# Gate and up products with tokens stationary and 512 weight columns moving, and TensorE transposes of the gated product

## The chip, the cores and the metric

The kernel runs on one core of one Trainium2 chip, in one launch. The metric is the device time of an execution in microseconds (us). TensorE (PE) multiplies matrices: one operand is loaded into the array and stands still (stationary), the other streams through it (moving). VectorE (DVE), ScalarE (ACT) and GpSimd (POOL) do the elementwise work, and SyncE (SP) issues most DMAs. Each engine has its own queue and takes its instructions in order.

## The reference

One layer of a hybrid encoder over 256 tokens of width 2048: two recurrent token mixers, cross attention over 256 memory tokens, and a gated feed forward of inner width 5632. Each part adds to the residual and ends in a layer norm. The change lies in the feed forward:

```python
def swiglu(h, wg, wu, wd):
    return (jax.nn.silu(h @ wg) * (h @ wu)) @ wd
...
        xa = memory_cross_attention(h, mem, xa_wq[l], xa_wk[l], xa_wv[l], xa_wo[l])
        h = layer_norm(ALPHA * h + xa, ln2_g[l], ln2_b[l])
        ff = swiglu(h, ffn_wg[l], ffn_wu[l], ffn_wd[l])
        h = layer_norm(ALPHA * h + ff, ln3_g[l], ln3_b[l])
```

`wg` and `wu` are 2048 x 5632, `wd` is 5632 x 2048, all float32.

## The kernel before

All large weights are streamed from memory once, in **units** of 128 partitions x 1024 columns (512 KB). For each unit `split_half` loads the raw float32 weights (L150, SP's queue, 4 buffers `raw`), rounds them to a high part `wh` on ACT (L153, 3 buffers), and subtracts to get the low part `wl` on DVE (L155, 3 buffers). The activations are kept as such pairs too (`xTh`, `xTl`: 16 pairs of tiles of 128 features x 256 tokens). A product is then three matmuls: high by high, high by low, low by high.

There are two forms of it. **`wstat`** (L164, L165, L168) has the weights stationary, 128 columns at a time, and 256 tokens moving. One unit is 8 tiles of the contraction for 128 output features, and so 24 matmuls of 256 moving columns: 16 that read `wh`, then 8 that read `wl`. The output has features on the partitions. **`xstat`** (L192, L193, L196) has 128 tokens stationary and 512 weight columns moving. One unit is two tiles of the contraction for 512 output features, for each of two halves of the tokens, and so 12 matmuls of 512 moving columns; the first four read `wh`, the next two `wl`, and then again for the other tokens. The output has tokens on the partitions.

The feed forward loops over 44 blocks of 128 inner features. For each it calls `wtile` (which calls `wstat`) for the gate and again for the up product (two units each, 176 in all), applies Silu on ACT (L888), multiplies on DVE (L890), and splits the product into the pair `fh`, `fl` (`split_to`: L201 on ACT, L202 on DVE). These lie with features on the partitions, which is how the down product needs its stationary operand: four calls of `xstat` over `wd`, 22 units each (88 in all), in which contraction tile k of `fh` and `fl` is read in rising k. `residual` (L782) and a closing layer norm follow.

Ahead of the feed forward stands the layer norm `g2`, `b2` (called LN2 below). It normalises `hres`, transposes it on PE in blocks of 128 x 128 into PSUM tiles `lnt` (L240, 4 buffers), scales into `lnfull` on DVE or ACT, and makes `xTh` and `xTl` tile by tile. `affine_rows` then multiplies `hres` by rows of gains that are broadcast by DMA into `gb` (L256, issued on ACT's queue, 2 buffers) on DVE (L258, L259); in the feed forward it is called after the second block, and nothing needs it before the down product ends.

A scheduler orders each engine's queue: `stream()` gives a unit's load and split the priority of the unit's place in the stream, so that the splits run about three units ahead of PE, as far as their buffers go. `defer(n, fn)` puts `fn` aside, and `passed`, called after each unit's matmuls, counts it down and issues it after n more units. Before the change only `wstat` calls `passed`.

Of the kernel before, what the change touches and what calls it, by code (L numbers as in the profile page):

```python
# [11 lines left out]
F32 = mybir.dt.float32  # L12
F32R = mybir.dt.float32r
# [5 lines left out]
P = 128  # L19
# [27 lines left out]
def trunk(ctx, tc, x, memT, vec, rows, consts, lruw, loraw, w_in, w_out, wq, wk, wv, wo, wgu, wd, out,  # L47
# [52 lines left out]

    # ---------------------------------------------------------------- constants
    vt = base.tile([P, NV], F32, name="vt")
# [41 lines left out]

    # ---------------------------------------------------------------- streamed products
    def split_half(src, hf):
# [32 lines left out]
    def xstat(srcs, xh, xl):  # L179
        pt = [new_acc(), new_acc()]  # L180
        n = len(srcs)
        for u, src in enumerate(srcs):
            for hf in range(2):
                h, l = split_half(src, hf)
                first = u == 0 and hf == 0
                last = u == n - 1 and hf == 1
                for tt in range(2):
                    ts = slice(tt * P, (tt + 1) * P)
                    for kk in range(2):
                        k = u * 4 + hf * 2 + kk  # L190
                        w = h[:, kk * 512:(kk + 1) * 512]
                        nc.tensor.matmul(pt[tt], xh[k][:, ts], w, start=(first and kk == 0), stop=False)  # L192
                        nc.tensor.matmul(pt[tt], xl[k][:, ts], w, start=False, stop=False)  # L193
                    for kk in range(2):
                        k = u * 4 + hf * 2 + kk
                        nc.tensor.matmul(pt[tt], xh[k][:, ts], l[:, kk * 512:(kk + 1) * 512],  # L196
                                         start=False, stop=(last and kk == 1))
        return pt
# [9 lines left out]

    # ---------------------------------------------------------------- layer norm
    def ln_stats(st, pre, tt, nb):  # L210
# [49 lines left out]

    # ================================================================ input norm
    h0_d = dram.tile([P, 2, 2048], F32, name="h0_d")
    xTh, xTl = pair_tiles(base, NK, "xT")
    # ================================================================ mixer
    ya_d = [dram.tile([P, T], F32, name=f"ya_d{k}") for k in range(NT)]
# [3 lines left out]
    with ExitStack() as mx:  # L269
# [13 lines left out]

        # ---- first memory keys while the input is normalised
        xt = boot.tile([P, 2, 2048], F32, name="xt")
# [50 lines left out]

        # ---- persistent buffers with zeroed parts
        bz = grp.tile([P, 2, 4, P], F32, name="bkz")
# [18 lines left out]

        # ---- low-rank inputs
        lo = [grp.tile([P, T], F32, name=f"lo{j}") for j in range(4)]
# [10 lines left out]
        def decay_rates(g, jp, rates):  # L370
            # ---- decay and in-context rate, two tiles
            if jp == 0:
# [52 lines left out]
        def tile_stage(g, j, i, u, fs, av, ev, dt, kr, bkt, sv, yb, gt):  # L425
# [3 lines left out]
            def key_direction():  # L429
                # even chunk: [r'|kk'], [k''|b']; odd chunk: [kk'|r'], [b'|k'']  # L430
                zk = z["k"]
# [77 lines left out]
        def recurrence(g, kkr, gt, bkt, sv, dm, yb, scr, scx, pace):  # L509
            # ---- (I + A_b)^-T  # L510
            gi = gt.rearrange("p i h c n -> p (i h) c n")
# [37 lines left out]
        def chunk_steps(g, kkr, gt, bkt, sv, dm, yb, gi):  # L549
# [23 lines left out]
            dump(f"ymat{g}", ymat)  # L573
            # ---- chunk recurrence
            smat = grp.tile([P, 512], F32, name="smat", tag="t2a")
            ott = grp.tile([P, 2, 512], F32, name="ott", tag="t4")
            ot = [ott[:, a] for a in range(2)]
            for c in range(4):
# [38 lines left out]
                nc.scalar.copy(ot[c // 2][p0:p0 + 64, :], pso[p0:p0 + 64, :])  # L617
            # ---- group norm by token
            for a in range(2):
# [155 lines left out]

    # ================================================================ attention
    mp = ctx.enter_context(tc.tile_pool(name="mps2", bufs=4, reuse_waits="tile", space=PSUM))
# [7 lines left out]
    with at:  # L785
# [12 lines left out]
        layer_norm(hres, st, "g1", "b1", mp, xTh, xTl, sm_, ("f0", "f1", "f2"))  # L798
        # memory keys and values
        mTh, mTl = pair_tiles(ap1, NK, "B")  # L800
# [78 lines left out]

    # ================================================================ feed forward  # L880
    with ExitStack() as fx:
        fp = fx.enter_context(tc.tile_pool(name="ffn", bufs=1, reuse_waits="tile"))
        fs_ = fx.enter_context(tc.tile_pool(name="ffs", bufs=2, reuse_waits="tile"))
        fh, fl = pair_tiles(fp, NF, "f")
        for f in range(NF):
            ag = wtile(wgu[2 * f], xTh, xTl)
            sg = fs_.tile([P, T], F32, name="fsg")
            last = nc.scalar.activation(sg, ag, AF.Silu)  # L888
            au = wtile(wgu[2 * f + 1], xTh, xTl)
            nc.vector.tensor_tensor(sg, sg, au, ALU.mult)  # L890
            split_to(sg, fh[f], fl[f])
            if f == 1:
                affine_rows(hres, 4, "gb2")
                dump("h2", hres)
# [53 lines left out]
def _layout(i):  # L948
# [47 lines left out]
    o["wo"] = _pack_x(a["xa_wo"][0])  # L996
    gu = np.stack([a["ffn_wg"][0].reshape(D, NF, P), a["ffn_wu"][0].reshape(D, NF, P)], axis=2)
    o["wgu"] = _pack_w(gu.reshape(D, 2 * DFF))
    o["wd"] = _pack_x(a["ffn_wd"][0])
# [23 lines left out]
```

## Time and profile before

| what | us |
|---|---|
| median of 3 runs (lowest, highest) | 2201.14 (2199.56, 2203.24) |
| span of the profiled execution, first to last instruction | 2197.7 |
| gate and up products, from LN2's first product to the first down product | 1429.6 to 1940.9 |
| down products | 1940.9 to 2180 |
| after the last product | 2180 to 2197.7 |

The runs are timed without the profile and lie 1.9 to 5.5 us above the profiled execution's span, which leaves out what lies before the first and behind the last instruction. A span that changes by some us is therefore set against the median by its difference. In the rows below, PE is a matmul and PEld the load of its stationary operand. A matmul's duration in a row is longer than its share of the engine, since the next one starts before it ends: the share is read from start to start. A matmul's names stand as `out<-moving,stationary`, and the shape at its end is the output's.

### The profile page before, as it was taken

What the parts mean: (1) busy time and instruction counts of PE and PEld (TensorE: products, weight loads), DVE (VectorE), ACT (ScalarE), POOL (GpSimd) and SP (SyncE); (2) the same over time, 40 slices, a digit from 0 to 9 for tenths busy, and PEclk for the clock granted to TensorE, in tenths of its full rate; (3) what the DMA queues carried; (4) which work ended last, traced back from release to release, by engine and by line L of the source; (5) the groups of instructions that cost most, each with busy time, mean ns of one, the idle gap of its engine ahead of it and who ended that gap; (6) DMA issues with size and microseconds to landing.
All of it is one profiled execution on the core that took longest, in us unless ns stands there. A gap on an engine that the chain in (4) does not pass through costs nothing.

```text
span 2197.7 us, 38943 instructions
## 1 busy us (share of the span) xinstructions
PE 2127.7 (97%) x15952; PEld 2004.9 (91%) x15952; DVE 1394.3 (63%) x2121; ACT 1031.9 (47%) x1442; POOL 102.8 (5%) x137
## 2 busy tenths in 40 slices
PE   7999999999999999989999999999999999999996
PEld 7999899999999999877988998799999999988885
DVE  7778676967695769567854555674444444444445
ACT  6646444554455445554544444354444444443332
POOL 1200010011001100200100000000000000000001
PEclk9999999999999999999999999999999999999998
DMA  8555445554555465467565545566555555555563
GB/s 301 186 166 172 140 130 171 177 153 139 176 168 154 139 180 183 123 223 247 183 206 194 165 140 165 190 198 200 184 182 183 184 184 183 182 188 194 192 193 124
DMA packets 149939, 392.41 MB, mean 179 GB/s; under 512 B 39296, under 2 KB 58624, under 8 KB 149248
## 3 DMA queue, kind: packets, MB, share of 16 engines
q1 hardware_dynamic: 137776, 368.81, 52.6%
q10 hardware_dynamic: 9296, 13.24, 2.4%
q0 software_dynamic: 2688, 7.87, 1.2%
q8 instruction: 125, 2.05, 0.4%
q14 instruction: 54, 0.44, 0.1%
HBM read 375.05 MB, written 10.62 MB: 175 GB/s over the span
## 4 chain that ended last, share of the span: by engine, by line
PE 82%; DVE 8%; DMA 6%; issue 2%; ACT 2%; ACTq 0%; POOL 0%; SPq 0%; DVEq 0%; POOLq 0%
PE acc L168 17%; PE acc L165 17%; PE acc L164 17%; PE acc L193 7%; PE acc L192 7%; PE acc L196 7%; DVE wl L155 3%; DVE pd L534 2%; DMA gb<-in_rows_dram 1%; PE mix L491 1%; DVE xi L537 1%; PE rec L590 1%; PE rec L615 1%; DMA bkz<-bk 1%; PE rec L597 1%
## 5 line engine op out<-in xcount | busy, mean ns | idle before, releaser
L155 DVE TENSOR_TENSOR wl<-raw,wh 128x1024 fp32r<-128x1024 f32 x656 | 800.7, 1222 | 581.9 <-ACT wh L153 539.7
L153 ACT CAST wh<-raw 128x1024 fp32r<-128x1024 f32 x656 | 687.4, 1049 | 869.6 <-PE acc L165 535.2
L164 PE MATMUL acc<-xTh,wh 128*128 128x256 f32 x3520 | 881.1, 287 | 1.5 <-DVE ge L694 0.8
L165 PE MATMUL acc<-xTl,wh 128*128 128x256 f32 x3520 | 875.7, 285 | 1.2 <-DVE xTl L248 0.8
L165 PEld LDWEIGHTS acc<-xTl,wh 128*128 128x128 f32 x3520 | 677.9, 193 | 4.5 <-DVE xTl L248 1.2
L164 PEld LDWEIGHTS acc<-xTh,wh 128*128 128x128 f32 x3520 | 677.3, 193 | 4.8 <-DVE ge L694 1.4
L168 PE MATMUL acc<-xTh,wl 128*128 128x256 f32 x3520 | 503.8, 284 | 1.3 <-DVE wl L155 1.3
L168 PEld LDWEIGHTS acc<-xTh,wl 128*128 128x128 f32 x3520 | 457.0, 192 | 3.6 <-DVE wl L155 2.1
L193 PE MATMUL acc<-wh,fl 128*128 128x512 f32 x352 | 136.9, 389 | 0.0
L192 PE MATMUL acc<-wh,fh 128*128 128x512 f32 x352 | 136.9, 389 | 0.0
L196 PE MATMUL acc<-wl,fh 128*128 128x512 f32 x352 | 108.4, 389 | 0.0
L196 PEld LDWEIGHTS acc<-wl,fh 128*128 128x128 f32 x352 | 66.1, 188 | 13.8
L193 PEld LDWEIGHTS acc<-wh,fl 128*128 128x128 f32 x352 | 66.1, 188 | 13.7
L192 PEld LDWEIGHTS acc<-wh,fh 128*128 128x128 f32 x352 | 66.0, 188 | 13.6
L534 DVE TENSOR_TENSOR pd<-xi,al 128x2 f32<-128x2 f32 (+30 forms) x124 | 63.0, 508 | 2.4
L603 POOL TENSOR_SCALAR dms<-ct,dm 128x128 f32<-128x128 f32 x48 | 39.1, 826 | 496.4 <-DVE smat L609 423.3
L890 DVE TENSOR_TENSOR fsg<-fsg,acc 128x256 f32<-128x256 f32 x44 | 18.5, 420 | 61.9 <-PE acc L168 61.4
L192 PE MATMUL acc<-wh,Ah 128*128 128x512 f32 x128 | 50.6, 395 | 0.0
L193 PE MATMUL acc<-wh,Al 128*128 128x512 f32 x128 | 50.6, 395 | 0.0
L192 PE MATMUL acc<-wh,oTh 128*128 128x512 f32 x128 | 49.9, 390 | 0.0
L193 PE MATMUL acc<-wh,oTl 128*128 128x512 f32 x128 | 49.8, 389 | 0.0
L193 PE MATMUL acc<-wh,Bl 128*128 128x512 f32 x128 | 49.8, 389 | 0.0
(267 smaller groups left out, 2265.4 us busy)
## 6 DMA issues: line engine op xcount, KB each, us to landing
raw<-in_w_in_dram SPq DMA_DIRECT2D x232, 512.0 KB, 4.0
raw<-in_wgu_dram SPq DMA_DIRECT2D x176, 512.0 KB, 4.7
raw<-in_wd_dram SPq DMA_DIRECT2D x88, 512.0 KB, 4.6
raw<-in_wk_dram SPq DMA_DIRECT2D x32, 512.0 KB, 4.8
raw<-in_w_out_dram SPq DMA_DIRECT2D x32, 512.0 KB, 5.3
raw<-in_wv_dram SPq DMA_DIRECT2D x32, 512.0 KB, 4.8
raw<-in_wq_dram SPq DMA_DIRECT2D x32, 512.0 KB, 4.1
raw<-in_wo_dram SPq DMA_DIRECT2D x32, 512.0 KB, 4.4
```

The lines of the kernel that those rows point to most:

```text
L153: nc.scalar.copy(h, raw)
L155: nc.vector.tensor_tensor(l, raw, h.bitcast(F32), ALU.subtract)
L164: nc.tensor.matmul(acc, w, xh[k], start=(k == 0), stop=False)
L165: nc.tensor.matmul(acc, w, xl[k], start=False, stop=False)
L168: mm = nc.tensor.matmul(acc, l[:, kk * P:(kk + 1) * P], xh[k], start=False, stop=(k == 15))
L192: nc.tensor.matmul(pt[tt], xh[k][:, ts], w, start=(first and kk == 0), stop=False)
L193: nc.tensor.matmul(pt[tt], xl[k][:, ts], w, start=False, stop=False)
L196: nc.tensor.matmul(pt[tt], xh[k][:, ts], l[:, kk * 512:(kk + 1) * 512], start=False, stop=(last and kk == 1))
L491: nc.tensor.matmul(ps[:, c * P:(c + 1) * P], bz[:, hh, c, :], kr[:, c, :], start=True, stop=True)
L534: nc.vector.tensor_tensor(pd[:, 0:nj, 0:t + 1], xi[:, 0:nj, 0:t + 1], al[:, 0:t + 1, t].rearrange("p (o s) -> p o s", o=1) .broadcast_to([ ...
L537: nc.vector.tensor_reduce(xi[:, 0:nj, t], pd[:, 0:nj, 0:t + 1], AX.X, ALU.add, negate=True)
L603: nc.gpsimd.tensor_scalar(dms[:, j * P:(j + 1) * P], smask, dm[:, j, c:c + 1], None, ALU.mult)
```

## The change

The gate and up products are made by `xstat` in 11 blocks of 512 inner features: 8 units for the gate, 8 for the up product. Silu and the product then work on tiles of 128 tokens x 512 features. Their result has tokens on the partitions and is turned on PE: `turn` transposes the two tiles in eight blocks of 128 x 128 into two PSUM tiles, and splits these into `fh` and `fl`, which are now 128 x 512 tiles for two contraction tiles each. `turn` is put aside with `defer(2, ...)`, and so `xstat` now calls `passed` after each unit. The weights are laid out accordingly on the host. The number of units, their size and their order of loading stay as they are.

```diff
@@ xstat
-                        nc.tensor.matmul(pt[tt], xh[k][:, ts], l[:, kk * 512:(kk + 1) * 512],
-                                         start=False, stop=(last and kk == 1))
+                        mm = nc.tensor.matmul(pt[tt], xh[k][:, ts], l[:, kk * 512:(kk + 1) * 512],
+                                              start=False, stop=(last and kk == 1))
+                passed(mm.ins)
@@ feed forward
-        fh, fl = pair_tiles(fp, NF, "f")
-        for f in range(NF):
-            ag = wtile(wgu[2 * f], xTh, xTl)
-            sg = fs_.tile([P, T], F32, name="fsg")
-            last = nc.scalar.activation(sg, ag, AF.Silu)
-            au = wtile(wgu[2 * f + 1], xTh, xTl)
-            nc.vector.tensor_tensor(sg, sg, au, ALU.mult)
-            split_to(sg, fh[f], fl[f])
-            if f == 1:
+        fhp = [fp.tile([P, 2 * T], F32R, name="fh", tag=f"fh{k}") for k in range(NF // 2)]
+        flp = [fp.tile([P, 2 * T], F32R, name="fl", tag=f"fl{k}") for k in range(NF // 2)]
+        fh = [fhp[k // 2][:, (k % 2) * T:(k % 2 + 1) * T] for k in range(NF)]
+        fl = [flp[k // 2][:, (k % 2) * T:(k % 2 + 1) * T] for k in range(NF)]
+
+        def turn(nb, sg):
+            for pr in range(2):
+                ps = mp.tile([P, 512], F32, name="mix", tag="mix")
+                for j in range(2):
+                    cs = slice((2 * pr + j) * P, (2 * pr + j + 1) * P)
+                    for tt in range(2):
+                        nc.tensor.transpose(ps[:, (2 * j + tt) * P:(2 * j + tt + 1) * P], sg[tt][:, cs], ident)
+                split_to(ps, fhp[2 * nb + pr], flp[2 * nb + pr])
+
+        for nb in range(NF // 4):
+            pg = xstat([wgu[nb, 0, u] for u in range(4)], xTh, xTl)
+            sg = []
+            for tt in range(2):
+                s = fs_.tile([P, 512], F32, name=f"fsg{tt}", bufs=1)
+                last = nc.scalar.activation(s, pg[tt], AF.Silu)
+                sg.append(s)
+            pu = xstat([wgu[nb, 1, u] for u in range(4)], xTh, xTl)
+            for tt in range(2):
+                nc.vector.tensor_tensor(sg[tt], sg[tt], pu[tt], ALU.mult)
+            defer(2, partial(turn, nb, sg))
+            if nb == 0:
                 affine_rows(hres, 4, "gb2")
@@ weights on the host
-    gu = np.stack([a["ffn_wg"][0].reshape(D, NF, P), a["ffn_wu"][0].reshape(D, NF, P)], axis=2)
-    o["wgu"] = _pack_w(gu.reshape(D, 2 * DFF))
+    o["wgu"] = np.ascontiguousarray(np.stack([_pack_x(a["ffn_wg"][0]), _pack_x(a["ffn_wu"][0])], axis=1))
```

The queues of all engines are the same up to LN2. Behind it they differ; three places follow. In these rows a name's last number is the scheduler's own.

The first place is PE's queue right behind LN2's first 14 transposes: of before, two accumulators (`acc_15914` gate, `acc_15977` up) of the first block.

```order
L164 MATMUL acc_15914<-xTh0_77,wh_15917 128x256
L164 MATMUL acc_15977<-xTh0_77,wh_15980 128x256
L165 MATMUL acc_15914<-xTl0_93,wh_15917 128x256
L164 MATMUL acc_15914<-xTh1_78,wh_15917 128x256
L165 MATMUL acc_15977<-xTl0_93,wh_15980 128x256
L165 MATMUL acc_15914<-xTl1_94,wh_15917 128x256
L164 MATMUL acc_15914<-xTh2_79,wh_15917 128x256
```

The same place of the change (`acc_15870` and `acc_15871` are the two halves of the tokens; `lnt` is LN2's seventh transpose and on):

```order
L192 MATMUL acc_15870<-wh_15874,xTh0_77 128x512
L192 MATMUL acc_15871<-wh_15874,xTh0_77 128x512
L193 MATMUL acc_15870<-wh_15874,xTl0_93 128x512
L192 MATMUL acc_15870<-wh_15874,xTh1_78 128x512
L193 MATMUL acc_15870<-wh_15874,xTl1_94 128x512
L196 MATMUL acc_15870<-wl_15876,xTh0_77 128x512
L196 MATMUL acc_15870<-wl_15876,xTh1_78 128x512
L193 MATMUL acc_15871<-wh_15874,xTl0_93 128x512
L241 MATMUL lnt_15750<-ct_67,hres_10531 128x128 x2
```

Before, the third contraction tile is wanted after six products of 256 columns; now a whole unit of twelve products of 512 columns needs tiles 0 and 1 alone.

The second place is PE's queue of the change at the first `turn`: the last two products of the second unit of block 1's gate, then the transposes (four into each `mix`, of which the first two of each stand here), then the third unit.

```order
L196 MATMUL acc_16229<-wl_16252,xTh2_79 128x512
L196 MATMUL acc_16229<-wl_16252,xTh3_80 128x512
L896 MATMUL mix_16266<-ct_67,fsg0_16016 128x128
L896 MATMUL mix_16266<-ct_67,fsg1_16018 128x128
...
L896 MATMUL mix_16273<-ct_67,fsg0_16016 128x128
L896 MATMUL mix_16273<-ct_67,fsg1_16018 128x128
...
L192 MATMUL acc_16228<-wh_16282,xTh4_81 128x512
```

Before, no transposes stand in the gate and up products: PE goes from one block's products straight to the next one's.

The third place is DVE's queue where `affine_rows` works on `hres`; of before (`fsg` and `fl` are block 1's product and its split):

```order
L258 TENSOR_TENSOR hres_10531<-hres_10531,gb_16192 128x256 x2
L890 TENSOR_TENSOR fsg_16102<-fsg_16102,acc_16104 128x256
L155 TENSOR_TENSOR wl_16296<-raw_16292,wh_16294 128x1024
L259 TENSOR_TENSOR hres_10531<-hres_10531,gb_16192 128x256 x2
L258 TENSOR_TENSOR hres_10531<-hres_10531,gb_16199 128x256 x2
L259 TENSOR_TENSOR hres_10531<-hres_10531,gb_16199 128x256 x2
L155 TENSOR_TENSOR wl_16326<-raw_16322,wh_16324 128x1024
```

The same of the change:

```order
L155 TENSOR_TENSOR wl_16044<-raw_16040,wh_16042 128x1024
L259 TENSOR_TENSOR hres_10531<-hres_10531,gb_16192 128x256 x2
L260 TENSOR_TENSOR hres_10531<-hres_10531,gb_16192 128x256 x2
L259 TENSOR_TENSOR hres_10531<-hres_10531,gb_16199 128x256 x2
L260 TENSOR_TENSOR hres_10531<-hres_10531,gb_16199 128x256 x2
L155 TENSOR_TENSOR wl_16062<-raw_16058,wh_16060 128x1024
L155 TENSOR_TENSOR wl_16080<-raw_16076,wh_16078 128x1024
```

In both, splits of weights (`wl`) are queued behind work that needs a `gb` from a DMA; in the change two pieces of `gb` stand between two splits, and no block's product among them.

## Rows read from the trace of the kernel before

**Rows 1.** The page: busy time by engine, and the chain that ended last, by engine.
```profile
PE 2127.7 (97%) x15952; PEld 2004.9 (91%) x15952; DVE 1394.3 (63%) x2121; ACT 1031.9 (47%) x1442; POOL 102.8 (5%) x137
...
PE 82%; DVE 8%; DMA 6%; issue 2%; ACT 2%; ACTq 0%; POOL 0%; SPq 0%; DVEq 0%; POOLq 0%
```

**Rows 2.** PE by stretches: length, busy (matmuls), clock, DMA share, GB/s.
```profile
1421.60:1429.60 8.00, 3.47 (x16) 0.63 0.43 137
1429.60:1445.40 15.80, 14.90 (x117) 0.97 0.30 92
...
1500.00:1900.00 400.00, 400.00 (x3335) 1.00 0.57 183
...
1940.80:2180.00 239.20, 239.20 (x1058) 1.00 0.56 183
```

**Rows 3.** Groups in 1421.6 to 1941: busy us, mean ns | idle before.
```profile
L164 PE MATMUL acc<-xTh,wh 128*128 128x256 f32 x1408 | 345.5, 283 | 0.0
...
L155 DVE TENSOR_TENSOR wl<-raw,wh 128x1024 fp32r<-128x1024 f32 x176 | 215.1, 1223 | 178.0 <-ACT wh L153 176.0 <-ACT fsg L888 1.9
...
L153 ACT CAST wh<-raw 128x1024 fp32r<-128x1024 f32 x177 | 185.4, 1047 | 265.0 <-PE acc L165 257.2 <-DMA raw<-in_wgu_dram 5.9 <-PE acc L193 1.7
```

**Rows 4.** PE in order of time at the last gate/up unit: start, length.
```profile
1937.10 1.12 PE L168 MATMUL acc<-xTh,wl 128*128 128x256 f32 x8
...
1939.98 1.12 PE L168 MATMUL acc<-xTh,wl 128*128 128x256 f32 x8
1940.94 0.40 PE L192 MATMUL acc<-wh,fh 128*128 128x512 f32 x1
```

**Rows 5.** Down products on L192: ns min/median/max, first and last start us.
```profile
L192 PE MATMUL acc<-wh,fh x352: 389/389/396, 1940.9 to 2179.4; 128*128 128x512 f32 x176
```

**Rows 6.** PE in order of time: four transposes amid `wstat` in the mixer.
```profile
804.23 0.60 PE L484 MATMUL mix<-ct,bk 128*128 128x128 f32 x4
804.59 0.36 PE L164 MATMUL acc<-xTh,wh 128*128 128x256 f32 x1
804.79 0.28 PE L165 MATMUL acc<-xTl,wh 128*128 128x256 f32 x1
```

**Rows 7.** PE in order of time through LN2.
```profile
1421.03 0.61 PE L196 MATMUL acc<-wl,oTh 128*128 128x512 f32 x2
1425.98 2.09 PE L240 MATMUL lnt<-ct,hres 128*128 128x128 f32 x8 [4.34 <-DVE hres L234]
...
1429.58 0.78 PE L164 MATMUL acc<-xTh,wh 128*128 128x256 f32 x2
...
1435.32 0.82 PE L240 MATMUL lnt<-ct,hres 128*128 128x128 f32 x6
1435.89 1.20 PE L168 MATMUL acc<-xTh,wl 128*128 128x256 f32 x8
...
1444.23 0.38 PE L165 MATMUL acc<-xTl,wh 128*128 128x256 f32 x1 [0.19 <-POOL xTl L248]
```

**Rows 8.** What PE waited for in 1421.6 to 1941: us, times, longest.
```profile
PE acc L165 <- DVE xTl L248: 0.5, 1, 0.5
PE acc L165 <- POOL xTl L248: 0.4, 2, 0.2
```

**Rows 9.** Who waited for the rows' DMA in 1420 to 1500: us, times.
```profile
  DVE hres L258: 6.1, 3
  DVE hres L259: 2.4, 2
```

**Rows 10.** ACT's queue, then DVE, in order of time: issue and first use.
```profile
1453.24 1.79 ACTq L256 DMA_DIRECT2D gb<-in_rows_dram  x4
...
1458.37 0.76 DVE L258 TENSOR_TENSOR hres<-hres,gb 128x256 f32<-128x256 f32 x2 [2.85 <-DMA gb<-in_rows_dram]
```

**Rows 11.** Groups by shape over the whole span: 128x512 out of PSUM.
```profile
L782 DVE SCALAR_TENSOR_TENSOR hres<-hres,acc 128x512 f32<-128x512 f32 x24 | 16.2, 676 | 4.9 <-PE acc L196 4.9
...
L202 DVE TENSOR_TENSOR vl<-acc,vh 128x512 fp32r<-128x512 f32 x8 | 5.5, 687 | 0.5
```

## The prediction

> **What bounds the kernel now.** I read the busy times and the chain of waits first: PE is busy 97% of the span and makes up 82% of the chain that ended last [rows 1]. The share alone says little, so I went on to the stretches of the feed forward. Through the steady gate and up products PE is busy 400.00 of 400 us at full clock (1.00, which is 2.4 GHz), and through the down products 239.20 of 239.20, while the DMA engines are used 0.56 to 0.57 [rows 2]. So in this stage time is what PE's instructions take from start to start. The only holes are at LN2: 3.47 of 8.00 and 14.90 of 15.80 us busy [rows 2].
>
> Next, how fast PE goes in each form, which is what the change swaps. In the steady gate and up stretch 3335 matmuls take 400 us, 119.9 ns each [rows 2]; in order of time, one unit's eight low products start at 1937.10 and the next unit's at 1939.98, so a unit of 24 takes 2.88 us, 120.0 ns each [rows 4]. The down products already have the new form. Of their 88 units, the first product starts at 1940.9, and the last on L192 (the ninth of the twelve of the last unit) at 2179.4 [rows 5]: 238.5 us for 87 units and 8/12, so 2.72 us a unit and 226.7 ns a matmul. Against 256 and 512 columns at 2.4 GHz (106.7 and 213.3 ns) each form pays the same 13.3 ns per matmul on top. The change halves the number of matmuls and so half of that surcharge goes.
>
> **The change part by part.** *Products.* 176 units stay 176 units. Each goes from 2.88 to 2.72 us: 176 x 0.16 = 28.2 us less. That PE can be fed at this rate is shown by the down products, with units of the same size, splits and loads, and no hole. The splits take DVE 1.22 and ACT 1.05 us of each unit [rows 3].
>
> The Trainium skill (TensorE: Matmul & The Clock Gate, section "Back-to-back issue gap") speaks against this term: it gives the warm gap of a matmul as N / 2.4 + 2.5 ns. By it, the 13.3 ns of the rows would be 2.5, and the products' gain only 176 x (24 x 109.2 - 12 x 215.8) ns = 5.5 us by estimate. The rows of this kernel at both widths disagree with it, and the sum goes by the rows.
>
> *Transposes.* 11 turns of eight. The mixer transposes plain float32 blocks of the same size on the same identity amid `wstat`: four start at 804.23, the next product starts at 804.59, and the one behind that 0.20 instead of 0.12 us later [rows 6]. That is 0.09 us each and 0.08 for the change of work, so 0.80 per turn; LN2's six at 1435.32 took 0.57, 0.095 each [rows 7]. 11 x 0.80 = 8.8 us. Bounds: 11 x 0.72 = 7.9 without the 0.08; above, the 14 of LN2 that ran after a pause at half clock took from 1425.98 to 1429.58 [rows 7], 0.257 us each, 22.6 us in all. PE has no pause ahead of a turn, so I take the warm rows.
>
> Does a turn wait for its data? Behind the up product DVE multiplies two tiles of 128 x 512 out of PSUM, about 0.68 us each [rows 11], with at most one `wl` of 1.22 us in the way: 2.6 us. Two units of products (5.44 us) stand ahead of the turn. The `mix` tiles have four buffers and a turn takes two, so its evacuation is not waited for either. The last turn falls behind the second down unit, where contraction tiles 0 to 3 are being read; tiles 40 to 43 are read last. The elementwise work becomes fewer, longer instructions on engines that wait for PE (DVE was idle 178.0 us before its splits alone [rows 3]): nothing. If that cover were gone, one turn's product and split would be 2 x 0.68 + 2 x 0.69 = 2.7 us on the path [rows 11].
>
> *LN2.* PE idles 4.34 us for the normalised rows, then transposes at half clock [rows 7]; both stay. From the first product at 1429.58 [rows 7] to the first down product at 1940.94 [rows 4] are 511.4 us, of which 176 x 2.88 = 506.9 are products. The other 4.5 are LN2's last 18 transposes (18 x 0.09 = 1.6), waits for `xTl` (0.5 + 0.4 [rows 8]) and about 2 for the cold start and for switching between the two kinds. With the new form a unit needs only the next two contraction tiles. LN2 delivers 16 tiles between 1429.58 and PE's last wait for one at 1444.23 [rows 7], 1.8 us for two, and a unit lasts 2.72, so from the second unit on the tiles are ahead of PE. I walked DVE's, ACT's and PE's queues of the change through these first units with the durations above and found no wait. I keep 2.2 of the 4.5: 2.3 us gained, with bounds of 0 and 4.5 - 1.6 = 2.9.
>
> *The rows of gains.* Here something is lost. `affine_rows` makes DVE wait for DMAs, 8.5 us in five waits before [rows 9], with splits queued behind it: four DMAs were issued from 1453.24, and DVE went on at 1458.37 [rows 10], 5.1 us later. Before, that cost PE nothing. In the new form the `wl` of a unit is wanted after four of twelve products, 0.91 us into the unit, where before it was wanted after 16 of 24, at 1.92: a us less of slack. By the walk, of the eight splits around the `gb` pieces three come within 0.2 us of being late, and one is late by about a us. I take 1.3 us, bounds 0 and 8.5 (all of DVE's wait uncovered).
>
> *Sum.* -28.2 + 8.8 - 2.3 + 1.3 = -20.4 us. The down products and the tail keep their length. The span goes from 2197.7 to 2177.3; the median of the runs shown, 2201.1, to 2180.7. I say 2181.
>
> **The rivals.**
> *Slow transposes.* They run as the 14 at half clock did: 22.6 us instead of 8.8, the sum is -6.6, and the time 2194.5. For it: those rows. Against it: both rows amid products at full clock. The Trainium skill (the same page, "Part 4: PE-mode transpose") gives about 275 ns for one in a kernel's context and says that the clock is not raised by them; by that estimate 88 cost 24.2 us and the time is 2196. The warm rows here (0.09) disagree, for transposes amid products.
> *The rows of gains uncovered.* All 8.5 us reach PE: the sum is -13.2, the time 2188. For it: the smaller slack. Against it: three split buffers.
> *The turn waits.* This is the one on the other side. The transposes stand in PE's own queue, and a late product of Silu and up stops all products behind them. It is a loss from the point where a turn waits 20.4 / 11 = 1.85 us, which is a product that is ready 7.3 us after its last matmul instead of 2.6; a wait of 4 us each gives -20.4 + 44 = +23.6 and 2225. For it: DVE takes its queue in order, and one split held up ahead of the product would do it. Against it: those splits' buffers come free before the up product ends.
> *No gain from width.* What a matmul pays above its columns' own time grows with its columns, so that halving the number saves nothing: the products' term is 0, the sum 0 + 8.8 - 1.0 = +7.8, and the time 2209. For it: only that these very products were never timed in the new form. Against it: the down products' 2.72 us a unit, with the same surcharge at twice the columns. By the page's gap, quoted above, little of the surcharge would be there to save: an estimate of 2203.
>
> **How the numbers follow.** A change under 0.2% (4.4 us, the spread of the runs shown) can't be told from none. The forecast has 0.83, within 2176 to 2186 by itself (transposes 7.9 to 10, LN2 0 to 2.9, gains 0 to 5, and 2 us of spread between runs). Rows of gains uncovered 0.07, slow transposes 0.05, the turn waits 0.03, no gain from width 0.02. The range takes in the second case and the spread: 2174 to 2190; about 1 in 10 is left out above and a few in 100 below. Faster: the first three, of which a little of the third falls within 0.2%: 0.94. Within: 0.03 (a weak form of the last two). Slower: 0.03.
>
> **What would show it.** Right: a gate and up unit of 2.72 us between turns; 0.7 to 0.9 us from a turn's first transpose to the next product, with no idle time before it; the first down product 1918 to 1922 us into the span, with ten turns ahead of it and one behind; the down products and the tail as long as now. Wrong: PE idle before the transposes with DVE's product as the releaser; PE idle before low products with `wl` as the releaser past the first block; a granted clock under 1.00 after LN2; a unit of 2.8 us or more.

## The result, and the profile after

| | us |
|---|---|
| before, median of 4 runs (lowest, highest) | 2201.45 (2199.56, 2203.24) |
| changed kernel, median of 4 runs (lowest, highest) | 2179.14 (2177.37, 2180.05) |
| ratio, 95% interval | 0.9898 [0.9884, 0.9912] |
| forecast | 2181, range 2174 to 2190 |

The kernel is 22.3 us faster, and the time lies 1.9 us from the forecast. The sum behind it did less well: two of its terms were off by 7 us together, and a gain that no step had foreseen made up for them. That the time came out so near is luck.

The page of the changed kernel, busy time by engine and the chain that ended last, beside [rows 1]:

```profile
PE 2109.7 (97%) x13928; PEld 1903.8 (87%) x13928; DVE 1391.6 (64%) x2077; ACT 1024.8 (47%) x1398; POOL 103.5 (5%) x137
...
PE 83%; DVE 8%; DMA 5%; issue 2%; ACT 1%; ACTq 0%; SPq 0%; POOL 0%; DVEq 0%; POOLq 0%
```

PE has 2024 matmuls fewer, DVE and ACT 44 instructions fewer each, and the shares hardly move. PE by stretches says more (length, busy, clock, DMA share, GB/s), beside [rows 2]: LN2's wait, the first gate products, a later hole and what follows it, the steady gate and up products, the down products.

```profile
1414.20:1422.30 8.10, 3.26 (x15) 0.83 0.43 133
1422.30:1426.00 3.70, 3.70 (x11) 0.50 0.05 14
1426.00:1432.00 6.00, 6.00 (x35) 0.97 0.32 91
1454.00:1458.00 4.00, 0.92 (x4) 0.88 0.39 95
1458.00:1462.00 4.00, 4.00 (x10) 0.50 0.59 145
1462.00:1466.00 4.00, 4.00 (x15) 0.77 1.00 414
1500.00:1900.00 400.00, 400.00 (x1802) 1.00 0.58 190
1920.40:2160.00 239.60, 239.60 (x1062) 1.00 0.56 182
```

The steady stretch is as forecast: full clock, no hole, 1802 matmuls where [rows 2] have 3335. Two stretches run at half clock (0.50, 1.2 GHz). One lies over the first gate products, where this profile of the kernel before ran at 0.97 [rows 2]; its second profile, below, has one there too, so this one is not the change's. The other lies behind a hole at 1454 to 1458, and neither profile of the kernel before has that. What PE waited for from 1414 to the end, beside [rows 8]:

```profile
PE lnt L241 <- DVE hres L235: 4.3, 1, 4.3
PE acc L196 <- DVE wl L155: 3.1, 1, 3.1
PE lnt L241 <- ACT hres L237: 0.3, 1, 0.3
PE lnt L241 <- DVE lnfull L246: 0.2, 1, 0.2
```

The waits for `xTl` are gone, no transpose waits for `fsg`, and one product waits 3.1 us for `wl`. A turn and the last products ahead of the down products, in order of time (two pieces):

```profile
1481.12 0.62 PE L196 MATMUL acc<-wl,xTh 128*128 128x512 f32 x2
1481.58 1.03 PE L896 MATMUL mix<-ct,fsg 128*128 128x128 f32 x8
1482.37 0.48 PE L192 MATMUL acc<-wh,xTh 128*128 128x512 f32 x1
1482.68 0.40 PE L193 MATMUL acc<-wh,xTl 128*128 128x512 f32 x1
...
1918.62 0.62 PE L196 MATMUL acc<-wl,xTh 128*128 128x512 f32 x2
...
1919.98 0.62 PE L196 MATMUL acc<-wl,xTh 128*128 128x512 f32 x2
1920.43 0.39 PE L192 MATMUL acc<-wh,fh 128*128 128x512 f32 x1
```

Half a unit, from one pair of low products to the next, takes 1.36 us, so a unit takes 2.72. A turn takes 0.79 to the next product, which is followed 0.31 later instead of 0.23: 0.87 in all. The first down product starts at 1920.43.

Set side by side from the start of the last product of the mixer's output weights (`wo`, the last ahead of LN2), the stages show where the 19.9 us between the two profiled spans came from:

| stage, us | before | changed | rows_pool (below) |
|---|---|---|---|
| last `wo` product starts | 1421.3 | 1414.0 | 1415.9 |
| from there to the first gate product | 8.3 | 8.3 | 7.7 |
| gate and up products | 511.4 | 498.1 | 491.8 |
| down products | 239.2 | 240.0 | 240.0 |
| last `wo` product to the end | 776.4 | 763.8 | 757.2 |

12.6 us were gained from the last `wo` product on, where the sum had 20.4; 7.3 us were gained ahead of it, where the queues of all engines are the same.

### The profile page after: what moved, and what is told of

The parts are those of the page before. It is cut to its first block, busy times and chain, and to the rows that moved or that the text cites. A ratio compares the mean times of both kernels' runs of the same rounds, so it can differ in the third digit from the quotient of the medians.

```text
span 2177.8 us, 34808 instructions
## 1 busy us (share of the span) xinstructions
PE 2109.7 (97%) x13928; PEld 1903.8 (87%) x13928; DVE 1391.6 (64%) x2077; ACT 1024.8 (47%) x1398; POOL 103.5 (5%) x137
## 3 DMA queue, kind: packets, MB, share of 16 engines
q8 instruction: 109, 1.79, 0.3%
## 4 chain that ended last, share of the span: by engine, by line
PE 83%; DVE 8%; DMA 5%; issue 2%; ACT 1%; ACTq 0%; SPq 0%; POOL 0%; DVEq 0%; POOLq 0%
PE acc L196 15%; PE acc L193 15%; PE acc L192 15%; PE acc L168 10%; PE acc L165 10%; PE acc L164 10%; DVE wl L155 3%; DMA gb<-in_rows_dram 2%; DVE pd L535 1%; PE mix L492 1%; DVE xi L538 1%; PE rec L591 1%; PE rec L616 1%; PE rec L598 1%; PE rec L650 1%
## 5 line engine op out<-in xcount | busy, mean ns | idle before, releaser
L164 PE MATMUL acc<-xTh,wh 128*128 128x256 f32 x2112 | 533.8, 289 | 1.5 <-DVE ge L695 0.8
L165 PE MATMUL acc<-xTl,wh 128*128 128x256 f32 x2112 | 527.4, 286 | 0.3 <-DVE xTl L249 0.3
L164 PEld LDWEIGHTS acc<-xTh,wh 128*128 128x128 f32 x2112 | 406.0, 192 | 4.6 <-DVE ge L695 1.0
L165 PEld LDWEIGHTS acc<-xTl,wh 128*128 128x128 f32 x2112 | 406.2, 192 | 2.9 <-DVE xTl L249 0.5
L168 PE MATMUL acc<-xTh,wl 128*128 128x256 f32 x2112 | 305.6, 285 | 0.8 <-DVE wl L155 0.8
L168 PEld LDWEIGHTS acc<-xTh,wl 128*128 128x128 f32 x2112 | 275.0, 192 | 2.7 <-DVE wl L155 1.2
L192 PE MATMUL acc<-wh,xTh 128*128 128x512 f32 x704 | 276.7, 393 | 0.0
L193 PE MATMUL acc<-wh,xTl 128*128 128x512 f32 x704 | 275.9, 392 | 0.0
L196 PE MATMUL acc<-wl,xTh 128*128 128x512 f32 x704 | 218.8, 392 | 3.1 <-DVE wl L155 3.1
L193 PEld LDWEIGHTS acc<-wh,xTl 128*128 128x128 f32 x704 | 133.2, 189 | 27.4
L192 PEld LDWEIGHTS acc<-wh,xTh 128*128 128x128 f32 x704 | 133.2, 189 | 27.3
L192 PE MATMUL acc<-wh,fh 128*128 128x512 f32 x352 | 137.0, 389 | 0.0
L192 PEld LDWEIGHTS acc<-wh,fh 128*128 128x128 f32 x352 | 66.1, 188 | 13.8
L196 PEld LDWEIGHTS acc<-wl,fh 128*128 128x128 f32 x352 | 66.1, 188 | 13.7
```

Source lines behind the costliest of these rows:

```text
L164: nc.tensor.matmul(acc, w, xh[k], start=(k == 0), stop=False)
L165: nc.tensor.matmul(acc, w, xl[k], start=False, stop=False)
L168: mm = nc.tensor.matmul(acc, l[:, kk * P:(kk + 1) * P], xh[k], start=False, stop=(k == 15))
L196: mm = nc.tensor.matmul(pt[tt], xh[k][:, ts], l[:, kk * 512:(kk + 1) * 512], start=False, stop=(last and kk == 1))
```

## The experiments

The kernel before was timed again beside each group of runs, and its median lay between 2198.8 and 2208.1 us. So each ratio is to the runs beside it, and stages are compared from the last `wo` product on.

**The rows of gains off DVE and ACT (rows_pool).** The 3.1 us wait is one for `wl`. DVE and ACT at that place, in order of time ("ACTq" is ACT's queue issuing DMAs):

```profile
1454.09 0.76 DVE L259 TENSOR_TENSOR hres<-hres,gb 128x256 f32<-128x256 f32 x2 [2.65 <-DMA gb<-in_rows_dram]
1455.80 0.76 DVE L260 TENSOR_TENSOR hres<-hres,gb 128x256 f32<-128x256 f32 x2 [0.95 <-DMA gb<-in_rows_dram]
1456.48 2.36 DVE L155 TENSOR_TENSOR wl<-raw,wh 128x1024 fp32r<-128x1024 f32 x2
```
```profile
1452.25 1.05 ACT L153 CAST wh<-raw 128x1024 fp32r<-128x1024 f32 x1 [2.62 <-DMA raw<-in_wgu_dram]
1452.35 5.06 ACTq L257 DMA_DIRECT2D gb<-in_rows_dram  x4
1457.51 1.04 ACT L153 CAST wh<-raw 128x1024 fp32r<-128x1024 f32 x1 [4.21 <-DMA gb<-in_rows_dram]
```

The DMAs of the next rows write buffers that DVE must first have read. ACT's queue stands 5.06 us at issuing four of them, with the next `wh` behind; DVE stands 2.65 and 0.95 us for the rows, with `wl` behind. PE starts again when the first `wl` is ready, and then at half clock:

```profile
1454.29 0.39 PE L193 MATMUL acc<-wh,xTl 128*128 128x512 f32 x1
1457.75 1.22 PE L196 MATMUL acc<-wl,xTh 128*128 128x512 f32 x2 [3.08 <-DVE wl L155]
1458.77 0.63 PE L192 MATMUL acc<-wh,xTh 128*128 128x512 f32 x1
1459.20 0.63 PE L193 MATMUL acc<-wh,xTl 128*128 128x512 f32 x1
```

The experiment moves this work to POOL, which is idle there, and to POOL's own DMA queue (`lowest` is LN2's last `xTl`):

```diff
-                    nc.scalar.dma_start(gb[:, n, :], rows[gi + n:gi + n + 1, s].broadcast_to([P, 256]))
+                    dq.dma_start(gb[:, n, :], rows[gi + n:gi + n + 1, s].broadcast_to([P, 256]))
...
-                    nc.vector.tensor_tensor(pre[:, tt, s], pre[:, tt, s], gb[:, 0, :], ALU.mult)
+                    eng.tensor_tensor(pre[:, tt, s], pre[:, tt, s], gb[:, 0, :], ALU.mult)
...
-                affine_rows(hres, 4, "gb2")
+                with tc.issue_after(lowest[0].ins):
+                    affine_rows(hres, 4, "gb2", nc.gpsimd, nc.gpsimd)
```

> The changed kernel with the second rows of gains (affine_rows after block 0) multiplied on POOL and loaded from POOL's queue, behind LN2's last xTl; DVE and ACT have none of it in their queues. Theory: the wait of 3.1 us for wl and the 5.5 us at half clock behind it (2.8 us lost) come from DVE's and ACT's queues standing behind gb. Then both are gone, PE has no wait for wl in the feed forward, and the time is 2179.1 - 5.9 = 2173.2, 2172 to 2175. Rival: the weights themselves come late, since the rows' DMAs and the two transfers of 1 MB for the last norm share the DMA engines with them. Then the wait stays, now with ACT waiting for raw, and the time is 2177 to 2180.

Measured: 2173.60 us (2171.53 to 2176.86), ratio to before 0.9884 [0.9864, 0.9904]. PE by stretches over the same place, of the changed kernel and then of rows_pool:

```profile
1440.00:1470.00 30.00, 26.92 (x106) 0.89 0.77 253
```
```profile
1440.00:1470.00 30.00, 30.00 (x133) 1.00 0.88 291
```

The wait and the half clock behind it are gone, and from the last `wo` product to the end the kernel takes 757.2 us. The changed kernel took 763.8, and 763.1 and 763.0 in the two more profiles below. At the first down product the two are 6.9 us apart, and 1.0 of it they are apart already at the fifth unit, where LN2 has ended: in rows_pool its transposes fall a little differently and less of the stretch is at half clock. So the rows of gains cost the new form about 6 us: 3.1 of waiting and 2.9 of half clock (4.0 us at 0.50 and 4.0 at 0.77). In the two more profiles PE waited 3.5 and 4.4 us there and then ran at half clock for 2.8 and 3.4 us; by the same comparison the rows cost 5.2 and 6.4.

**The same on the kernel before (rows_pool_old).**

> The kernel before, with the rows of gains (their four pairs of DMAs and their products) on POOL behind the last xTl, where rows_pool has them. Theory (the rows cost PE something only in the new form, where wl is wanted 0.91 us into a unit): the gate and up products keep their 511 to 512 us and the time stays within 2 us of before's 2199. Rival (they cost either form the same, so the change lost nothing by them): gate and up 505 to 507, and 5 to 6 us less, about 2193, as rows_pool gained on the changed kernel.

Measured: 2203.55 us (2201.5 to 2209.71) against 2206.22 for before beside it, ratio 0.999 [0.998, 1.0]. The gate and up products took 512.1 us, as in before (511.4, and 512.1 in again_before); the mark ahead of LN2 lies 2.4 us earlier (table below), and that is about the difference of the times. The rows of gains cost the old form nothing on PE: the change itself made them dear, as the prediction argued from the smaller slack.

**Each transpose twice (turn_twice).**

```diff
-                    for tt in range(2):
+                    for tt in (0, 1, 0, 1):
                         nc.tensor.transpose(ps[:, (2 * j + tt) * P:(2 * j + tt + 1) * P], sg[tt][:, cs], ident)
```

> The changed kernel with each turn's eight transposes made twice into the same places (16 a turn); all other queues are the same. It measures a turn's price. By the warm rows, 0.09 us each and nothing new at the edges: 88 x 0.09 = 7.9 us more, 2187.0, 2186 to 2188.5. If a transpose cost what LN2's at half clock do (0.257), 22.6 us more, 2201.7. If part of the turns were hidden behind something else, less than 6 us more.

Measured: 2186.82 us (2184.1 to 2194.97), ratio to before 0.994 [0.9922, 0.9957]. A doubled turn in order of time:

```profile
1577.87 1.91 PE L896 MATMUL mix<-ct,fsg 128*128 128x128 f32 x16
1579.53 0.47 PE L192 MATMUL acc<-wh,xTh 128*128 128x512 f32 x1
```

Sixteen take 1.66 us, 0.104 each, where eight took 0.79, 0.099 each; the eight added cost 0.87. The gate and up products grew by 7.0 us for 80 transposes, less than 80 x 0.109 = 8.7, since in this profile the rows of gains cost two waits of 1.8 us and no half clock. So the total came out as expected, but the price per transpose in it (7.0 / 80) is too low, and the expectation of new_long below took that price over.

**PE kept busy ahead of LN2 (best).** This is rows_pool with products of data at hand in PE's 4.3 us wait:

```diff
+        with tc.issue_after(final[0].ins):     # the last wo product
+            ps = mp.tile([P, 512], F32, name="warmps", tag="mix")
+            for r in range(34):
+                nc.tensor.matmul(ps[:, 0:T], oTh[0][:, 0:P], oTh[1], start=True, stop=True)
```

> rows_pool with 34 products of 128 x 256 between the last wo product and LN2's transposes on PE, in the 4.3 us that PE waits there; their results are unused. Theory (the idle PE ahead of LN2 is what drops the clock, and the first gate products still run at half clock for it): granted clock 1.00 through LN2's transposes and the first products, the first gate product 1 to 2 us earlier, and from the last wo product to the end 754 to 755.5 instead of 757.2: 2171. Rival (the first products wait for xTh and xTl, whatever the clock): less than 1 us, 2173.

Measured: 2175.48 us (2175.35 to 2175.98), ratio to before 0.9862 [0.9843, 0.9881]. PE by stretches, of rows_pool and then of best:

```profile
1416.00:1421.00 5.00, 0.67 (x5) 0.99 0.55 195
1421.00:1424.10 3.10, 2.94 (x12) 0.50 0.07 26
```
```profile
1417.06:1421.50 4.44, 4.24 (x35) 1.00 0.58 180
1421.50:1424.00 2.50, 1.73 (x12) 1.00 0.30 113
1424.00:1426.00 2.00, 2.00 (x14) 1.00 0.02 4
1426.00:1432.00 6.00, 5.63 (x32) 1.00 0.11 29
```

The half clock is gone and the first gate product comes 7.2 us behind the last `wo` product instead of 7.7, yet the length to the end is 757.0 against 757.2. Both cases were right in part. PE waits 1.2 us for LN2's tiles, as the rival had it, but the fifth unit still starts 21.4 us behind the last `wo` product instead of 22.3, 1.0 us earlier. That gain is lost again behind LN2. ACT stands 5.06 us for weights (`raw`) that land late, with the DMA engines busy 0.98 of the time from 1445 to 1455, and PE stands for the `wh` that ACT makes of them:

```profile
1454.12 1.05 ACT L153 CAST wh<-raw 128x1024 fp32r<-128x1024 f32 x1 [5.06 <-DMA raw<-in_wgu_dram]
```
```profile
1455.22 0.50 PE L194 MATMUL acc<-wh,xTh 128*128 128x512 f32 x1 [0.55 <-ACT wh L153]
```

From the twelfth unit on both kernels are level; in rows_pool ACT stands 4.1 us for `raw` at this place, and PE not at all. So the idle PE ahead of LN2 does drop the clock, at a price of about 1 us, and here the loading of weights takes that back. That the time is 1.9 us above rows_pool's, and above both cases, lies ahead of LN2 (table below).

**Both kernels once more, unchanged (again_before, again_after).**

> The kernel before, profiled once more; the question is the stretch ahead of LN2, in which both kernels have the same queues on every engine and the changed kernel's trace is 7.2 us shorter (its last product of wo's stage starts at 1413.8 where it was at 1421.0). If that stretch varies from execution to execution, as waits for the recurrence's small DMAs might, this profile has the last wo product some us away from 1421.0, nearer to 1414 to 1418 perhaps, and a span that moves with it. If it belongs to the program (where its tensors and instructions lie in memory), the last wo product starts at 1421 within 1.5 us again and the span is 2197 to 2200.

> The changed kernel, profiled once more. If the stretch ahead of LN2 varies from execution to execution, the last wo product moves by some us from 1413.8; if it belongs to the program, it stays within 1.5 us. Behind it the same on both views: from LN2's first product to the first down product 498 us within 2, with one wait of PE for wl of about 3 us some 36 us behind LN2's first product and half the clock for about 5 us after it.

Measured: again_before 2205.2 us, again_after 2179.87, one run each. From the last `wo` product to the end 777.1 and 763.1 us; the last `wo` product at 1426.0 and 1415.0. again_before's mark fits neither case of its expectation: it moved 5 us, and away from the changed kernel's. again_after's pause was 2.9 us as expected, the half clock behind it shorter (2.8 us for 5). The lengths from the last `wo` product on repeat within 0.7 us, and the gain ahead of LN2 is there again. The six runs that follow ask what it comes with.

The half clock over the first gate products moves from one execution to the next. It covers 4.0 us of them in the changed kernel and again_after, 1.0 in after_third (below), 0.9 in before and 3.5 in again_before. The stretches of after_third and again_before:

```profile
1420.83:1426.00 5.17, 5.17 (x28) 0.90 0.12 35
```
```profile
1434.37:1438.00 3.63, 3.63 (x19) 0.52 0.07 20
```

**The shape of the weights (old_reshaped).** Kernel before:

```diff
-            ag = wtile(wgu[2 * f], xTh, xTl)
+            ag = wtile(wgu[f // 4, f % 4 // 2, 2 * (f % 2)], xTh, xTl)
...
-    o["wgu"] = _pack_w(gu.reshape(D, 2 * DFF))
+    o["wgu"] = _pack_w(gu.reshape(D, 2 * DFF)).reshape(11, 2, 4, P, 2048)
```

> The kernel before, with wgu declared as a tensor of 11 x 2 x 4 x 128 x 2048, as the change has it; the same bytes in the same order, and the same queues on every engine. Theory A (the shape of the input sets the 7 us that the change gained ahead of LN2): the last wo product at about 1414 us instead of 1421, the time about 2192. Theory B (it is the program, or where it lies, and not this tensor): 1421 and 2199 as before.

Measured: 2208.18 us, ratio to before 1.0001 [0.9988, 1.0015]. Not the shape.

**The number of instructions (padded).** Changed kernel:

```diff
+        spare = fp.tile([P, 1], F32, name="spare")
+        with tc.issue_after(lowest[0].ins):
+            for r in range(4135):
+                nc.gpsimd.memset(spare, 0.0)
         for nb in range(NF // 4):
```

> The changed kernel with 4135 stores of one column on POOL behind LN2's last xTl, where POOL has nothing to do, so that the program has as many instructions as that of before; their results are unused. Theory A (the 7 us ahead of LN2 come with a shorter program): the last wo product at about 1421 us and the time about 2186. Theory B (the number of instructions has no part in it): 1414 and 2179. Where the stores hold up something behind LN2, that shows from the last wo product on, where the changed kernel takes 763.5 us.

Measured: 2179.51 us, ratio to before 0.988 [0.9862, 0.9898]. Not the number of instructions as such, when the added ones are on POOL.

**PE's program shorter and longer (old_short, new_long, and after_third beside them).** old_short, then new_long:

```diff
-        for f in range(NF):
+        for f in range(NF // 2):
...
-            pt = xstat([wd[nb, u] for u in range(11)], fh, fl)
+            pt = xstat([wd[nb, u] for u in range(11)], fh[:NF // 2] * 2, fl[:NF // 2] * 2)
```
```diff
-                    for tt in range(2):
+                    for tt in (0, 1) * 24:
                         nc.tensor.transpose(ps[:, (2 * j + tt) * P:(2 * j + tt + 1) * P], sg[tt][:, cs], ident)
```

> The kernel before with 22 of the 44 blocks of the gate and up products left out (the down product reads the 22 that are made twice): 2112 matmuls fewer, so that PE's program is as short as the changed kernel's (13840 matmuls against 13928); the queues up to LN2 stay. Theory A (what the change gains ahead of LN2 comes with a shorter program for PE): the last wo product at 1413 to 1417 us, and from the times (less the part behind it, which the profile gives) the same. Theory B (PE's program length has no part in it): as far behind the changed kernel's as before is, 1421 to 1428. Behind LN2 the leaving out takes 22 x 4 x 2.88 = 253 us off in either case.

> The changed kernel with each transpose of a turn made 24 times, 2024 matmuls more, so that PE's program is as long as that of before (15952 matmuls). Theory A: the last wo product at 1421 to 1428 us. Theory B: at 1413 to 1417 as in the changed kernel. Behind LN2 the transposes add 2024 x 0.0875 = 177 us by what they cost in turn_twice (7.0 us for 80), or more, up to 0.107 each = 217 us, if a long run of them goes slower.

> The changed kernel once more, for the stage ahead of LN2 beside before, old_short and new_long in the same call: before's median moved from 2199 to 2206 us between two calls. If the changed kernel moves with it (a property of the hour or of where memory lies), it comes out near 2184 to 2187 where before is at 2206; if only the longer program moves, it stays at 2178 to 2181.

Measured: old_short 1938.97 us, new_long 2411.96 (ratio 1.093 [1.0906, 1.0953]), after_third 2180.7 (ratio 0.9883 [0.9861, 0.9904], before beside it 2208.1). The table gives where the last `wo` product starts. "Mean" is the mean of the timed runs' spans less the kernel's own length from there to the end, which its profile gives (for before 776.7, the mean of its two profiles). Single executions scatter: by their spans the mark lies at 1421.4 to 1432.7 in before beside the last three of the table, 1411.9 to 1418.3 in old_short, 1421.1 to 1430.6 in new_long and 1412.5 to 1422.1 in after_third, five runs each of the changed ones.

| kernel | PE matmuls | last `wo`, profile | mean | before, beside it |
|---|---|---|---|---|
| rows_pool | 13928 | 1415.9 | 1414.9 | 1420.7 |
| turn_twice | 14016 | 1421.4 | 1414.1 | 1420.7 |
| rows_pool_old | 15952 | 1425.2 | 1425.6 | 1428.0 |
| old_reshaped | 15952 | 1420.8 | 1426.8 | 1428.0 |
| padded | 13928 | 1417.3 | 1415.7 | 1428.0 |
| best | 13962 | 1416.8 | 1416.8 | 1428.0 |
| old_short | 13840 | 1416.6 | 1415.0 | 1427.7 |
| new_long | 15952 | 1428.2 | 1425.6 | 1427.7 |
| after_third | 13928 | 1412.5 | 1416.3 | 1427.7 |

Theory A held in both directions (old_short also leaves out loads and splits; new_long adds to PE alone). By the means, the old form with a short program for PE starts LN2 as early as the changed kernel, 12.7 us ahead of before; the changed form with PE's program made as long as before starts it 9.3 us later than after_third, though all that was added to it runs behind LN2 and on PE alone.

The profiles say where the time goes, without the subtraction. PE's 1000th matmul starts at 141 to 145 us in all fourteen profiles of this document. The 7000th, still in the mixers, starts at 850.6 to 855.1 us in the five with 15952 matmuls and at 841.6 to 849.3 in the nine with fewer, and behind it the distance hardly changes (8.1 us by the means there, 8.3 at the last `wo` product). Up to the 7000th PE waited 29.1 to 33.1 us in the five and 23.8 to 28.6 in the nine, and the stretches at half clock add up to 10.2 to 17.1 us and 3.4 to 13.7. By the means, longer waits are 4.8 of the 8.1 us, and 5.4 us more at half clock, where half of the time is lost, about 2.7.

PE's program goes through a DMA queue of its own: these are the rows of the instruction queue (packets, MB, share) and of one of the small transfers ahead of LN2 (us from issue to landing) for before, the changed kernel, old_short and new_long.

```profile
q8 instruction: 125, 2.05, 0.4%
bkz<-bk POOLq DMA_DIRECT2D x32, 128.0 KB, 4.2
```
```profile
q8 instruction: 109, 1.79, 0.3%
bkz<-bk POOLq DMA_DIRECT2D x32, 128.0 KB, 3.7
```
```profile
q8 instruction: 108, 1.77, 0.4%
bkz<-bk POOLq DMA_DIRECT2D x32, 128.0 KB, 3.5
```
```profile
q8 instruction: 125, 2.05, 0.3%
bkz<-bk POOLq DMA_DIRECT2D x32, 128.0 KB, 4.4
```

2.05 MB over before's 31904 matmuls and weight loads and 1.79 MB over the changed kernel's 27856 are both 64 bytes each, so this queue is PE's. With the shorter program the `bkz` transfer lands some tenths of a us earlier: its median is 3.1 to 3.8 us in the nine profiles and 3.8 to 4.5 in the five. Round trips of such transfers stand on the path there (DMA has 5% of the chain, in [rows 1] 6%), but PE's waits for it are only 5.0 us in before and 3.8 in the changed kernel, and two other small transfers (`scr<-gt`, `al<-scr`) land no later with the longer program. By 1400 us both kernels had moved the same 83 packets of PE's queue, so it is not the traffic up to there. Why a longer program slows a stage that runs long before its end stays open.

**PE's program shorter still (new_short).** Changed kernel:

```diff
-        for nb in range(NF // 4):
+        for nb in range(2):
...
-            pt = xstat([wd[nb, u] for u in range(11)], fh, fl)
+            pt = xstat([wd[nb, u] for u in range(11)], fh[:8] * 6, fl[:8] * 6)
```

> The changed kernel with 9 of its 11 blocks of the gate and up products left out (the down product reads the 8 contraction tiles that are made, again and again): PE's program has 12128 matmuls instead of 13928. The two runs before this one showed that the stage ahead of LN2 goes with the length of PE's program (about 10 us for 2024 matmuls). If it goes in proportion, the last wo product comes at 1404 to 1410 us here; if it is a step somewhere between 13962 and 15952 matmuls, it comes at 1412 to 1417 as in the changed kernel. Behind LN2 the leaving out takes 9 x (16 x 2.72 + 0.87) = 399.5 us off.

Measured: 1778.0 us (1773.04 to 1782.42); the last `wo` product at 1414.4 in the profile, which was the longest of the five runs, and at 1409.7 by the mean of five, with before at 1425.2 beside it. One number speaks for a step and the other for proportion: inconclusive.

## Why the prediction was right, and where not

*Products: right.* 176 units at 2.72 us, 28.2 us less, with PE 400.00 of 400 us busy. The Trainium skill's gap of N / 2.4 + 2.5 ns (TensorE: Matmul & The Clock Gate, "Back-to-back issue gap"), which that section gives for a matmul by itself, is not what these products pay: by it the gain would have been 5.5 us by estimate, and start to start they take 226.7 ns at 512 columns.

*Transposes: right, 9.6 us for 8.8.* 11 x 0.87. No turn waited, and the last one fell among the down products, which grew by 0.8. The slow rival is out. Its price was a little high, too: the 0.257 us that it took for a transpose at half clock held a wait of 0.19 us, and the last six, from 1428.26 to 1429.58, took 0.22 each. The Trainium skill's 275 ns for a transpose in context ("Part 4: PE-mode transpose", same page) is what one lasts here from start to end, not what it costs, as the group of all turns ahead of the down products shows (mean ns behind the comma), while eight of them start within 0.79 us:

```profile
L896 PE MATMUL mix<-ct,fsg 128*128 128x128 f32 x80 | 10.4, 272 | 0.0
```

*LN2: the size was wrong.* I had 2.3 us gained. The waits for `xTl` did go, but what the first four units take beyond their products' own time hardly fell. In the changed kernel the fifth unit starts 14.96 us behind the first gate product; less 48 x 0.2267 = 10.88, 4.1 are left. In before four units take 15.7 us, and less 96 x 0.12 = 11.5, 4.2 are left. The step that failed is "I keep 2.2 of the 4.5", and in it the "about 2 for the cold start and for switching", which were let go almost whole. The start of the fifth unit in the changed kernel and in after_third:

```profile
1437.29 0.39 PE L192 MATMUL acc<-wh,xTh 128*128 128x512 f32 x1
```
```profile
1434.58 0.39 PE L192 MATMUL acc<-wh,xTh 128*128 128x512 f32 x1
```

In after_third, whose first gate product starts at 1420.83, only 2.9 are left. There 1.0 us of the stretch is at half clock, as in before (0.9), where in the profile of the changed kernel it is 4.0. again_before, with 3.5, has 4.8 left. So with the half clock in the same place the change gains about 1.3 us here (4.2 against 2.9), and 0.7 or so with it late (4.8 against 4.1); the 2.3 that I had were not seen. What is left can be estimated from rows: 18 transposes (1.7 us at 0.095), six changes from transposes to products (0.5 at 0.08) and half of the time at half clock (0.5 or 2.0) make 2.7 and 4.2.

*The rows of gains: the mechanism was right, the size wrong.* The late `wl` was foreseen ("one is late by about a us", 1.3 us, bounds 0 and 8.5). It was late by 3.1, since ACT's queue was held at its DMAs too, and the half clock behind the pause, which no step had counted, doubled it: 6.0 (5.2 and 6.4 in the kernel's two other profiles).

*The sum* from the last `wo` product on is thus -28.2 + 9.6 - 0.1 + 6.0 = -12.7, and 12.6 were measured. With that alone the time would have been about 2188.5, inside the range but near the rival of the rows uncovered, and 7.5 us from the forecast. One of the prediction's signs of being wrong did show, a granted clock under 1.00 after LN2 (0.50 behind the pause). One of its signs of being right, the first down product at 1918 to 1922 us, held only through the gain ahead of LN2: without the 7.3 us it would have been 1927.7.

*Ahead of LN2: not forecast.* The sum took this stage as unchanged because its queues are. It gave 7.3 us between the two profiled executions, and 22.3 - 12.6 = 9.7 between the medians. With PE's program as long as before it goes away, and without any of the change's products it is there: it comes with the number of instructions on PE, which the change cut by 13%. Through what is open. That it is about as large as what the other terms missed is chance.

## What to carry to other kernels

A form with fewer, longer matmuls wants both halves of a split sooner: look for small work on the splitting engines, and for DMA issues that wait for a buffer in front of a cast, and move it to an idle engine and queue. Count the half clock behind a new pause of PE with the pause; in the profile shown it cost as much again (2.9 us for 3.1), in others less. When a change shortens a program, compare stages from a common mark and not spans alone: a gain ahead of the change can cover a miss inside it. And before a stretch at half clock is put down to a change, see in a second profile of each kernel whether it stays where it was.

## What the runs showed of the hardware

The length of PE's program moved a stage that is long over before the added part runs, by about 10 us for some 2000 matmuls and their loads, in both directions (12.7 us earlier in old_short than in before, 9.3 later in new_long than in after_third); 4135 more instructions on POOL did not.

At the rows of gains, pauses of PE of 2.93, 3.08, 3.50, 3.70 and 3.90 us (again_after, the changed kernel, after_third, new_long, new_short) were each followed by a stretch at 0.50; one of 2.64 in padded and two of 1.8 in turn_twice were not.

Transposes in a long run stay at full clock and go no faster: in new_long 192 of them took from 1753.62 to 1774.50, 0.109 us each, and the stretch 1700 to 1710, which held 94 of such a run, had a granted clock of 1.00 (PE busy is the first pair of numbers, the clock the third from the end). With them the added 2024 cost 221 us, above both prices that had been expected.

```profile
1753.62 21.12 PE L896 MATMUL mix<-ct,fsg 128*128 128x128 f32 x192
1774.50 0.47 PE L192 MATMUL acc<-wh,xTh 128*128 128x512 f32 x1
...
1700.00:1710.00 10.00, 10.00 (x95) 10.00 (x93) 0.69 (x1) 0.38 (x1) 0.00 (x0) 1.00 0.01 2
```
